# Weaving the feed-forward's down units into its up units, and twelve more seven-product units

## The chip, the core and the metric

The kernel runs on one core of a Trainium2 chip, with float32 inputs and outputs in HBM. The metric is the device time of one execution in microseconds (us). The engines are named as in the profile: PE (matrix products; PEld loads its stationary operand), DVE (vector), ACT (scalar), POOL, and SP, which issues most of the transfers. Each takes its own instructions strictly in the order written here, since the kernel is scheduled by hand; semaphores tie the engines together.

## What is computed

A decoder trunk of two layers over 256 tokens of width 2048. Each layer is a mixer (pooling in layer 0, attention in layer 1), a normalization, a gated feed-forward network with a short causal convolution, and another normalization:

```python
def conv_ffn(h, w_up, conv_w, conv_b, w_down):
    u = h @ w_up                          # 256x2048 @ 2048x11008
    up = jnp.pad(u, ((0, 0), (CONV_WIDTH - 1, 0), (0, 0)))
    c = conv_b + up[:, 0:S] * conv_w[0]
    for j in range(1, CONV_WIDTH):
        c = c + up[:, j:j + S] * conv_w[j]
    gate, val = jnp.split(c, 2, axis=-1)
    return (jax.nn.silu(gate) * val) @ w_down     # 256x5504 @ 5504x2048

def reference(x, ...):
    ...
        h = layer_norm(DEEPNORM_ALPHA * h + mix, ln1_g[i], ln1_b[i])
        ff = conv_ffn(h, ffn_w_up[i], ffn_conv_w[i], ffn_conv_b[i], ffn_w_down[i])
        h = layer_norm(DEEPNORM_ALPHA * h + ff, ln2_g[i], ln2_b[i])
```

The attention's masks depend on distances between tokens alone (three dilated windows), not on the inputs.

## The kernel before

**Units.** All large products are cut into units, kept in the list `units` and worked through by `run_units`. A unit is one block of weights of up to 512 rows by 512 columns (1 MB): SP loads it into `raw` (three buffers, line 72), ACT rounds it into `wh` (L82), DVE forms the rest `wl` (L83), and PE multiplies both by the activations, which are split in the same way. `wh` and `wl` have four buffers, so a unit's split can start once PE begins the unit three places ahead of it; `ahead(i)` writes the splits of units up to i+3 and the loads of units up to i+5 into the queues before unit i's matmuls. After these, `run_units` writes the functions that `later(n, fn)` has put off by n units, then the unit's own `post`. So "one step later" means "behind the next unit's split" on DVE and ACT.

**Up units.** A group of four up units (`group`, `mm_quad`, L165 and L166, tile `acc`) makes 512 features of the gate half or the value half, in four of the eight PSUM banks. Quads q = 0 to 10 each have a gate group and a value group (`up`). Then `evac` (L577, L578) empties the banks into `u` through the temporary `ut`, `conv` makes three taps in three steps (L586, L591, L592), the gate gets its sigmoid and product (L615, L616), and the value is multiplied by the gate (L670) and split into `gq[q]` by `split_act` (L287, L283).

**Down units.** The second matrix is taken in four chunks of quads, `chunks` = (0,1,2), (3,4,5), (6,7), (8,9,10), in token-major form by `down` and `group_tm`. Each chunk makes four groups c, one for each 512 output columns, with one item for each quad. A plain item (`mk`, `go_t`, L235 to L237, tile `t`) is 24 matmuls of 512 columns. A seven-product item replaces the eight block products of a 2x2 by 2x2 block product by seven, with sums of blocks: 42 matmuls of 256 columns (L224 to L226, tiles `t` and `s`), in two units "a" and "b" that share one load. `split_sums` makes the sums of the weight blocks in `raw` on DVE (L104, L107 to L109) along with their splits (L103, L106, L96, L97). `left_sums(q)` makes the sums of the activation blocks once for each q (L645 to L648, L654, L656) in one of two sets of buffers, A and B. Which quads take seven products is in `sevens`: q = 1, 2, 4, 5, 6 in layer 0, and also 7, and half of the groups of 9, in layer 1. That is 46 items. After a group, `early_post` and `tm_post` (L791 to L821) combine its four banks into the residual `HT`; part of that goes by accumulating DMAs from POOL (L268).

**Order.** The three first quads' up groups come first. From then on whole down groups stand between whole up groups: gates 3, group 0 of chunk 0, values 3, group 1, gates 4, group 2, values 4, group 3, then quad 5, and the same with chunk 1 between quads 6 and 7. Chunk 2's groups follow values 8, gates 9, values 9 and gates 10. The last chunk comes behind values 10: `add_last` in layer 0, token-major with an alternating order (`turns`) in layer 1. `free[q]` and `done[q]` name the unit behind which quad q's split and convolution may be written.

**Masks.** `masks(i)` (L1118 to L1132) makes three 128x128 tables with POOL's iota and ten DVE operations each, at units 61, 63 and 65 of layer 0's feed-forward stage; the attention's scores read them.

Of the kernel before, what the change touches and what calls it, by code (L numbers as in the profile page):

```python
# [9 lines left out]
F32 = mybir.dt.float32  # L10
# [22 lines left out]
def trunk(ctx: ExitStack, tc: tile.TileContext, x, pool_w_in, pool_w_grp, pool_scale, pool_w_out,  # L33
# [14 lines left out]
    def bank(nm):  # L48
        return psp.tile([P, 512], F32, name=nm, tag="ps")
# [40 lines left out]
    def split_sums(i, kind):  # L90
        h = wh[i] = wp.tile([P, 4, 512], F32R, name=f"wh{i}", tag="wh")
        l = wl[i] = wp.tile([P, 4, 512], F32R, name=f"wl{i}", tag="wl")
        if kind == "b":
            r = raw.pop(i - 1)
            for n in (N2, N1):
                A.copy(h[:, :, n], r[:, :, n])  # L96
                V.tensor_tensor(l[:, :, n], r[:, :, n], h[:, :, n].bitcast(F32), OP.subtract)  # L97
            return
        r = raw[i]
        r11, r12, r21, r22 = r[:, B1, N1], r[:, B1, N2], r[:, B2, N1], r[:, B2, N2]  # L100
# [3 lines left out]
        V.tensor_tensor(r12, r12, r11, OP.subtract)  # L104
# [3 lines left out]
        V.tensor_tensor(r21, r21, r22, OP.subtract)  # L108
        V.tensor_tensor(r11, r22, r11, OP.subtract)  # L109

# [78 lines left out]
    def group_tm(w, r0s, c0, ncol, xqs, post, apart=False, seven=(), early=None):  # L189
        ps, held = [], []  # L190

        def leave():
            early(*ps[2:4])

        opening, closing = (min(seven), max(seven)) if seven else (None, None)

        def mk_seven(kind, j):
            fst, fin, op, cl = j == 0, j == len(r0s) - 1, j == opening, j == closing

            def go(h, l):  # L200
# [38 lines left out]
        def mk(j):  # L239
            def go(h, l):  # L240
                if j == 0:
                    ps.extend([bank("t0"), bank("t1")])
                    if apart:
                        ps.append(bank("t2"))
# [51 lines left out]
    onesd = const.tile([P, P], F32, name="onesd")  # L296
    one1 = const.tile([P, P], F32, name="one1")
# [4 lines left out]
    cnt = const.tile([P, 3, P], F32, name="cnt")  # L302
    negm = const.tile([P, 3, P], F32, name="negm")

# [243 lines left out]
    def ffn(lay):  # L548
# [16 lines left out]
        def evac(ps, nb, mode):  # L565
# [3 lines left out]
            def tmp():  # L569
                return fp.tile([P, T], F32, name="ut", tag="t1", bufs=4)  # L570

# [53 lines left out]
        def left_sums(q, s):  # L625
            pool, tag = (hp, "h") if q in (2, 5, 7) else (lnp, "sq")
            two = pool.tile([P, 2, 2, 2, P], F32R, name="xs01", tag=tag)
# [4 lines left out]
            if q in (2, 5, 7):  # L632
                one = apart()
            else:
                one = pools["ffn"].tile([P, 2, 2, P], F32R, name="xs2", tag="xs", bufs=1)
                one = [one[:, 0], one[:, 1]]
# [28 lines left out]
        def val_chain(q, nb, mode, ps):  # L665
# [21 lines left out]

        def up(q, mid, end):
            nb = min(4, NF - 4 * q)
            x0 = q == 0  # L690
            mode = "x" if x0 else "ab"
            group(w_up, rows4, 512 * q, nb * P, psrcs if x0 else xsrcs, gate_post(q, nb, mode),
                  mode=mode)
            for g in mid:
                units.extend(g)
            group(w_up, rows4, FF + 512 * q, nb * P, xsrcs, val_post(q, nb, "ab"))
            for g in end:
                units.extend(g)

        def down(n, last):  # L700
            qs = order[chunks[n][0]]
            rows = [(512 * q, min(512, FF - 512 * q)) for q in qs]
# [11 lines left out]
        for q in range(3):  # L714
            up(q, (), ())
# [12 lines left out]
        free[9] = len(units) - 5  # L728
        mark = len(units)
# [78 lines left out]
    def tm_post(lay, n, c):  # L808
# [3 lines left out]
        def post(t, ps, half=None):  # L812
# [11 lines left out]
            if c == 0 and t == 0:  # L824
                ST["bn"] = lnp.tile([P, 2, 8, 6], F32, name="bn", tag="bn")
            for i in range(2) if half is None else (half,):
# [121 lines left out]
    def scores(hq, ms):  # L948
        ap = pools["attn"]
        for m in ms:  # L950
# [6 lines left out]
            s = two[:, m % 2]  # L957
            sf, nf, cf = (t.rearrange("p a b -> p (a b)") for t in (s, negm, cnt))
            V.scalar_tensor_tensor(sf, ps[:, :3 * P], scale, nf, op0=OP.mult, op1=OP.add)
# [8 lines left out]
        for m in ms:  # L968
            s, mx, _ = pr[hq, m]
            sf, cf = (t.rearrange("p a b -> p (a b)") for t in (s, cnt))  # L970
            for t, sl in parts:
# [64 lines left out]

    with tc.tile_pool(name="start", bufs=1) as stp:
        for q in range(NQ):
            for t in range(2):
# [73 lines left out]
    with tc.tile_pool(name="ffn0", bufs=4) as fp:  # L1113
        pools["ffn"] = fp


        def masks(i):
            two = fp.tile([P, 2, P], F32, name="dist", tag="t1", bufs=4)  # L1118
# [3 lines left out]
            itwo = fp.tile([P, 2, P], I32, name="idist", tag="t1", bufs=4)  # L1122
            idist, im = itwo[:, 0], itwo[:, 1]
            cn = cnt[:, i, :]
            V.tensor_copy(idist, dist)
# [5 lines left out]
            V.scalar_tensor_tensor(cn, dist, 0.0, cn, op0=OP.is_ge, op1=OP.mult)  # L1131
            V.tensor_scalar(negm[:, i, :], cn, 0.0, NEG, op0=OP.is_equal, op1=OP.mult)  # L1132

        for i in range(3):
            later(61 + 2 * i, lambda i=i: masks(i))
        run_units(marks[1])
    with tc.tile_pool(name="attn", bufs=1) as ap:
        pools["attn"] = ap
        run_units(marks[2])
# [32 lines left out]
```

## Time and profile before

| | |
|---|---|
| three runs | 2040.13, 2040.58, 2041.29 us; median 2040.58 |
| the profiled execution | 2042.79 us, of which 2041.0 us is the span from the first to the last instruction |
| granted PE clock, mean | 0.998 |
| layer 0's feed-forward up to its last chunk | 218 to 869 us of the span |
| attention stage | 933 to 1317 us |
| layer 1's feed-forward up to its last chunk | 1317 to 1966 us |
| DVE and ACT busy over the span | 1648.8 us (81%), 1235.0 us (61%) |
| loads of one 1 MB block, issue to landing | 5.0 to 5.5 us, median by tensor |

The profile is of one execution. A window row gives, for a stretch of time, the busy time and number of instructions of each engine, the granted PE clock, the share of the DMA engines and GB/s. A timeline row gives the start, the duration (us), engine, line, operation, tiles, and in brackets the idle time of the engine before it with what ended it. Matmuls overlap, so the price of one is the distance from its start to the next start, not its duration; the same holds to a smaller degree for DVE and ACT, whose recorded durations reach some 0.1 us into the next instruction.

### The profile page before, as it was taken

Reading aid. Unit: us, or ns where it says so; the run is one execution under the profiler, and the core shown is the slowest. Engines: PE = TensorE matmul, PEld = TensorE weight load, DVE = VectorE, ACT = ScalarE, POOL = GpSimd, SP = SyncE. Lnnn points to the kernel's source line nnn. Section 1 sums busy time; section 2 is a strip of 40 time slices with the busy share of each in tenths; the row PEclk is TensorE's granted clock in tenths of the full one; section 3 lists DMA queues with packets and bytes.
Section 4 is the critical chain, followed back from the end, with each engine's and each line's share of the span. In section 5 each row is a group of like instructions: output and inputs, shape, how many; then the busy total and the mean of one; then the engine's idle time right before and its main releaser. Section 6 shows DMA issues by size and latency. Waiting matters only on the chain. (4 is left out here: it accounts for less than half of the span.)

```text
span 2041.0 us, 30664 instructions
## 1 busy us (share of the span) xinstructions
PE 2029.8 (99%) x12316; PEld 1805.3 (88%) x12316; DVE 1648.8 (81%) x1973; ACT 1235.0 (61%) x1634; POOL 75.2 (4%) x112
## 2 busy tenths in 40 slices
PE   9999999999999999999999999999999999999999
PEld 8898988889889888889888888998898889889987
DVE  6859877988998888889755667787888878889998
ACT  5544686656766575657444344587765666567662
POOL 2000000000000001100000000000001000000100
PEclk9999999999999999999999999999999999999999
DMA  8655567656665667865556555557667646765764
GB/s 255 208 202 189 166 209 212 189 195 215 205 194 189 219 211 199 239 217 162 187 193 202 176 170 176 178 188 224 185 187 230 223 147 227 216 196 177 221 209 167
DMA packets 278302, 405.88 MB, mean 199 GB/s; under 512 B 80414, under 2 KB 95668, under 8 KB 277904
## 3 DMA queue, kind: packets, MB, share of 16 engines
q1 hardware_dynamic: 266144, 389.72, 58.4%
q0 software_dynamic: 11584, 13.55, 4.4%
q8 instruction: 96, 1.57, 0.3%
q10 hardware_dynamic: 432, 0.66, 0.1%
q14 instruction: 46, 0.38, 0.1%
HBM read 380.01 MB, written 2.10 MB: 187 GB/s over the span
## 5 line engine op out<-in xcount | busy, mean ns | idle before, releaser
L165 PE MATMUL acc<-xc,wh 128*128 128x512 f32 x3264 | 1150.3, 396 | 0.0
L166 PE MATMUL acc<-xc,wl 128*128 128x256 f32 x3264 | 915.9, 281 | 0.4 <-DVE wl L83 0.4
L83 DVE TENSOR_TENSOR wl<-raw,wh 128x2048 fp32r<-128x2048 f32 (+2 forms) x330 | 713.8, 2171 | 238.8 <-ACT wh L82 233.0
L82 ACT CAST wh<-raw 128x2048 fp32r<-128x2048 f32 (+2 forms) x330 | 596.5, 1814 | 279.7 <-PE acc L165 136.5
L165 PEld LDWEIGHTS acc<-xc,wh 128*128 128x128 f32 x3264 | 615.9, 189 | 144.7 <-DVE o L1024 0.6
L166 PEld LDWEIGHTS acc<-xc,wl 128*128 128x128 f32 x3264 | 615.4, 189 | 0.9 <-DVE wl L83 0.7
L96 ACT CAST wh<-raw 128x1024 fp32r<-128x1024 f32 x92 | 93.3, 1050 | 146.5 <-PE acc L165 69.4
L97 DVE TENSOR_TENSOR wl<-raw,wh 128x1024 fp32r<-128x1024 f32 x92 | 108.8, 1219 | 38.6 <-ACT wh L96 38.5
L103 ACT CAST wh<-raw 128x1024 fp32r<-128x1024 f32 x92 | 72.2, 834 | 49.8 <-PE acc L165 42.9
L586 ACT ACTIVATE c<-u,cv 128x256 f32<-128x256 f32 x172 | 89.6, 593 | 12.5 <-DVE f L648 8.2
L577 ACT COPY ut<-acc 128x256 f32<-128x256 f32 x164 | 56.3, 371 | 67.4 <-PE acc L166 67.2
L236 PE MATMUL t<-wl,g 128*128 128x512 f32 (+1 forms) x243 | 93.9, 387 | 1.9 <-DVE wl L83 1.9
L235 PE MATMUL t<-wh,g 128*128 128x512 f32 (+1 forms) x243 | 94.6, 389 | 0.8 <-ACT wh L82 0.8
L237 PE MATMUL t<-wh,g 128*128 128x512 f32 (+1 forms) x243 | 94.0, 387 | 0.0
L268 POOL DMA_DIRECT2D ht<-w x24 | 20.3, 848 | 1842.9 <-DVE ht L817 1106.6
L106 DVE TENSOR_TENSOR wl<-raw,wh 128x1024 fp32r<-128x1024 f32 x92 | 83.7, 951 | 0.2 <-ACT wh L103 0.2
L591 ACT ACTIVATE a<-u,cv 128x256 f32<-128x256 f32 x172 | 73.4, 498 | 7.0 <-DVE g L656 7.0
L578 DVE TENSOR_TENSOR u<-acc,ut 128x256 f32<-128x256 f32 x164 | 60.2, 414 | 21.0 <-ACT ut L577 21.0
L225 PE MATMUL t<-wl,g 128*128 128x256 f32 x272 | 76.4, 281 | 0.0
L224 PE MATMUL t<-wh,g 128*128 128x256 f32 x272 | 76.4, 281 | 0.0
L226 PE MATMUL t<-wh,g 128*128 128x256 f32 x272 | 76.3, 281 | 0.0
L591 ACT ACTIVATE u<-u,cv 128x256 f32<-128x256 f32 x172 | 73.4, 499 | 0.0
(274 smaller groups left out, 3398.1 us busy)
## 6 DMA issues: line engine op xcount, KB each, us to landing
raw<-in_ffn_w_up_dram SPq DMA_DIRECT2D x160, 1024.0 KB, 5.1
raw<-in_ffn_w_down_dram SPq DMA_DIRECT2D x80, 1024.0 KB, 5.2
raw<-in_pool_w_out_dram SPq DMA_DIRECT2D x16, 1024.0 KB, 5.0
raw<-in_shared_w_k_dram SPq DMA_DIRECT2D x16, 1024.0 KB, 5.0
raw<-in_attn_w_q_dram SPq DMA_DIRECT2D x16, 1024.0 KB, 5.2
raw<-in_shared_w_v_dram SPq DMA_DIRECT2D x16, 1024.0 KB, 5.3
raw<-in_attn_w_o_dram SPq DMA_DIRECT2D x16, 1024.0 KB, 5.0
raw<-in_pool_w_in_dram SPq DMA_DIRECT2D x12, 1024.0 KB, 5.5
```

What stands on the lines that cost most here:

```text
L82: A.copy(wh[i][:, s], r[:, s])
L83: V.tensor_tensor(wl[i][:, s], r[:, s], wh[i][:, s].bitcast(F32), OP.subtract)
L96: A.copy(h[:, :, n], r[:, :, n])
L97: V.tensor_tensor(l[:, :, n], r[:, :, n], h[:, :, n].bitcast(F32), OP.subtract)
L106: V.tensor_tensor(l[:, k, n], r[:, k, n], h[:, k, n].bitcast(F32), OP.subtract)
L165: PE.matmul(ps[m], h[:, k, c], q[:, k, :, :T], start=st, stop=False)
L166: PE.matmul(ps[m][:, :T], l[:, k, c], q[:, k, 0, :T], start=False, stop=sp and not shifted)
L235: PE.matmul(to, xh, h[:, k, c], start=j == 0 and k == 0, stop=False)
L236: PE.matmul(to, xh, l[:, k, c], start=False, stop=False)
L237: PE.matmul(to, xl, h[:, k, c], start=False, stop=j == len(r0s) - 1 and k == nk - 1)
L586: A.activation(c[:, m, :], u[:, m, 2:], AF.Identity, scale=cv[:, 2, j:j + 1], bias=cv[:, 3, j:j + 1])
L591: A.activation(to[:, m, :], u[:, m, i:i + T], AF.Copy, scale=cv[:, i, j:j + 1])
```

## The change

The order of the work is changed, and `sevens` is larger. A down group is no longer a block between two up groups: `weave` puts its items between the units of one up group. With three items the order is item, up, item, up, item, up, up; with two it is item, up, up, item, up, up. A seven-product item keeps its units a and b together. The four banks of a down group are opened at its first item (`opened`). Chunk 2's groups now go with values 8, gates 9, values 9 and gates 10.

Quads 1 to 7 take seven products in both layers (9 as before), so there are 58 such items: quads 3 and 7 in layer 0 and quad 3 in layer 1 are new. A third set C of buffers for the left sums is made in the feed-forward's pool. Room for it comes from the mask tables, which are now tiles of the attention stage, made there at steps 6 to 8, from one buffer less for `ut`, and from two small tiles that share or leave their place. `split_sums` does two subtractions in one instruction, and `left_sums` turns the sign of one sum to match. In layer 1 the convolution of the last value group is put off by one unit.

```diff
@@ split_sums
         V.tensor_tensor(r22, r22, r12, OP.subtract)
-        V.tensor_tensor(r21, r21, r22, OP.subtract)
-        V.tensor_tensor(r11, r22, r11, OP.subtract)
+        both = r[:, :, N1].rearrange("p (b k) n -> p b k n", b=2)
+        V.tensor_tensor(both, both, r22.unsqueeze(1).to_broadcast([P, 2, 2, 256]), OP.subtract)
@@ group_tm
+        def opened():
+            ps.extend([bank("t0"), bank("t1")])
+            if seven:
+                ps.extend([bank("s2"), bank("s3")])
...
                 if kind == "a" and fst:
-                    ps.extend([bank("t0"), bank("t1")])
-                if kind == "a" and op:
-                    ps.extend([bank("s2"), bank("s3")])
+                    opened()
@@ ffn
-        order = {0: (0, 1, 2), 3: (3, 4, 5), 6: (6, 7) if lay == 1 else (7, 6), 8: (8, 9, 10)}
         every = (0, 1, 2, 3)
-        sevens = {1: every, 2: every, 4: every, 5: every, 6: every}
+        sevens = {q: every for q in range(1, 8)}
+        sets = {1: "A", 2: "B", 3: "C", 4: "A", 5: "B", 6: "A", 7: "BC"[1 - lay], 9: "A"}
         if lay == 1:
-            sevens.update({7: every, 9: (0, 2)})
-        free, done = {}, {}
+            sevens[9] = (0, 2)
+        free = {}
...
-                return fp.tile([P, T], F32, name="ut", tag="t1", bufs=4)
+                return fp.tile([P, T], F32, name="ut", tag="t1", bufs=3)
@@ left_sums
+            where = sets[q]
+            fp = pools["ffn"]
+            pool, tag = {"A": (lnp, "sq"), "B": (hp, "h"), "C": (fp, "xsc")}[where]
...
-            V.tensor_tensor(d[2], a11, a21, OP.subtract)
+            V.tensor_tensor(d[2], a21, a11, OP.subtract)
@@ val_chain
-            after(done.get(q, state["done"] + (0 if q in (2, 5, 10) else 1)), lambda: conv(u, NF + 4 * q, nb, valued, q == 10))
+            after(state["done"] + (0 if q in (2, 5) or (q == 10 and lay == 0) else 1), lambda: conv(u, NF + 4 * q, nb, valued, q == 10))
@@ ffn, the order
+        def weave(us, ks):
+            items = []
+            for k in ks:
+                if len(k) > 3 and k[3] == "b":
+                    items[-1].append(k)
+                else:
+                    items.append([k])
+            last = None
+            for i, u in enumerate(us):
+                j = i if len(items) > 2 else i // 2 if i % 2 == 0 else len(items)
+                if j < len(items):
+                    units.extend(items[j])
+                    last = len(units) - 1
+                units.append(u)
+            return last
...
         for n in (0, 1):
             d = down(n, False)
             q = chunks[n + 1][0]
-            up(q, d[:1], d[1:2])
-            up(q + 1, d[2:3], d[3:])
-            free[q] = done[q + 1] = len(units) - 1
+            for us, ks in zip(up(q) + up(q + 1), d):
+                free[q] = weave(us, ks)
             if n == 0:
-                up(q + 2, (), ())
+                for us in up(q + 2):
+                    units.extend(us)
         d = down(2, False)
-        up(8, (), d[:1])
-        up(9, d[1:2], d[2:3])
-        up(10, d[3:], ())
-        free[9] = len(units) - 5
+        gates8, vals8 = up(8)
+        units.extend(gates8)
+        gates10, vals10 = up(10)
+        for us, ks in zip((vals8,) + up(9) + (gates10,), d):
+            free[9] = weave(us, ks)
+        units.extend(vals10)
@@ masks, now behind the opening of the attention's pool
+        for nm in ("cnt", "negm"):
+            ST[nm] = ap.tile([P, 3, P], F32, name=nm)
...
         for i in range(3):
-            later(61 + 2 * i, lambda i=i: masks(i))
-        run_units(marks[1])
+            later(6 + i, lambda i=i: masks(i))
```

More of the change, by code (lines that the diff above doesn't have):

```diff
@@ L241, in go @@
                 if j == 0:
-                    ps.extend([bank("t0"), bank("t1")])
+                    opened()
                     if apart:
@@ L686, in at, with up @@
             later(max(u - state["done"], 1), fn)
-        def up(q, mid, end):
+        def up(q):
             nb = min(4, NF - 4 * q)
@@ L691, in up @@
             mode = "x" if x0 else "ab"
+            mark = len(units)
             group(w_up, rows4, 512 * q, nb * P, psrcs if x0 else xsrcs, gate_post(q, nb, mode),
                   mode=mode)
-            for g in mid:
-                units.extend(g)
             group(w_up, rows4, FF + 512 * q, nb * P, xsrcs, val_post(q, nb, "ab"))
-            for g in end:
-                units.extend(g)
+            us = units[mark:]
+            del units[mark:]
+            return us[:4], us[4:]
+        def weave(us, ks):
[13 more added lines that the diff above has]
+            return last
         def down(n, last):
-            qs = order[chunks[n][0]]
+            qs = range(*chunks[n])
             rows = [(512 * q, min(512, FF - 512 * q)) for q in qs]
@@ L714, in ffn @@
         for q in range(3):
-            up(q, (), ())
+            for us in up(q):
+                units.extend(us)
         for n in (0, 1):
@@ L1114, in trunk @@
         pools["ffn"] = fp
+        run_units(marks[1])
+    with tc.tile_pool(name="attn", bufs=1) as ap:
+        pools["attn"] = ap
+        for nm in ("cnt", "negm"):
+            ST[nm] = ap.tile([P, 3, P], F32, name=nm)
         def masks(i):
-            two = fp.tile([P, 2, P], F32, name="dist", tag="t1", bufs=4)
+            two = ap.tile([P, 2, P], F32, name="dist", tag="t1", bufs=2)
             dist, fm = two[:, 0], two[:, 1]
```

28 lines of the change are left out of this document (12 added, 16 removed).

## The prediction

> **What bounds the kernel now.** I read the totals first, then who waits for whom on PE, then the timeline of PE for prices, then windows over single stages, and last the timelines of DVE and ACT where DVE is fullest.
>
> ```profile
> PE 2029.8 (99%) x12316; PEld 1805.3 (88%) x12316; DVE 1648.8 (81%) x1973; ACT 1235.0 (61%) x1634; POOL 75.2 (4%) x112
> ```
>
> The waits of PE, in us in total, how often, and the longest:
>
> ```profile
> PE t L236 <- DVE wl L83: 1.9, 1, 1.9
> ...
> PE t L235 <- ACT wh L82: 0.8, 1, 0.8
> ```
>
> PE is busy for all of the span and waits for others for a few us in total. So time is saved by giving PE less to do, and lost where DVE and ACT can no longer keep ahead of it. What a down item costs PE is the distance between starts:
>
> ```profile
> 1672.79 0.39 PE L235 MATMUL t<-wh,g 128*128 128x512 f32 x1
> ...
> 1678.38 0.28 PE L224 MATMUL s<-wh,g 128*128 128x256 f32 x1
> ...
> 1683.34 0.28 PE L224 MATMUL s<-wh,g 128*128 128x256 f32 x1
> ```
>
> The first pair of starts is a plain item (5.59 us), the second a seven-product item, a and b (4.96). How full DVE is beside them:
>
> ```profile
> 551.50:589.50 38.00, 38.00 (x239) 34.04 (x238) 33.89 (x44) 29.54 (x46) 0.00 (x0) 1.00 0.45 146
> 589.50:627.40 37.90, 37.90 (x238) 33.95 (x237) 32.15 (x36) 24.18 (x32) 2.61 (x3) 1.00 0.66 207
> ...
> 1890.30:1922.70 32.40, 32.40 (x215) 29.56 (x214) 31.03 (x36) 23.35 (x35) 2.58 (x3) 1.00 0.69 203
> ```
>
> The numbers after the stretch's length are PE, PEld, DVE, ACT and POOL. The second row is one up group and one down group of a plain and two seven-product items (32.15 us of DVE in 37.9); the first is the same while the left sums of quad 5 are made; the third is four up units and two seven-product items in layer 1, where DVE is idle for only 32.40 - 31.03 = 1.4 us and PE still runs through. DMA at 0.45 to 0.69 has room.
>
> **The change, part by part.** *Twelve more seven-product items* (quads 3 and 7 in layer 0, quad 3 in layer 1, four groups each): 12 x (5.59 - 4.96) = **-7.6 us** on PE, which sets the end.
>
> *Weaving* by itself takes no matmul away. What it can save is the waits that are there now because a whole down group drains DVE's lead:
>
> ```profile
> 1857.14 0.40 PE L165 MATMUL acc<-xc,wh 128*128 128x512 f32 x1
> 1857.95 0.38 PE L166 MATMUL acc<-xc,wl 128*128 128x256 f32 x1 [0.42 <-DVE wl L83]
> ...
> 1976.78 0.28 PE L226 MATMUL s<-wh,xs 128*128 128x256 f32 x1
> 1977.88 0.50 PE L235 MATMUL t<-wh,g 128*128 128x512 f32 x1 [0.83 <-ACT wh L82]
> 1980.27 0.50 PE L236 MATMUL t<-wl,g 128*128 128x512 f32 x1 [1.89 <-DVE wl L83]
> ```
>
> ```profile
> 1977.50:1980.94 3.44, 1.17 (x4) 0.77 (x5) 3.44 (x3) 3.22 (x4) 0.00 (x0) 1.00 0.00 0
> 1980.94:1984.35 3.41, 3.41 (x10) 2.66 (x9) 3.41 (x3) 1.39 (x2) 0.00 (x0) 0.50 0.78 262
> ```
>
> At 1857, behind layer 1's first group of two seven-product items, the distance is 0.81 us; a 512-column matmul costs a 24th of a plain item, 0.23. With chunk 2's items apart this goes: -0.6. At 1977, behind layer 1's last value group, the distances are 1.10 and 2.39 against 0.12 (a 42nd of 4.96) and 0.23, so 3.1 us are lost, and then 3.41 us run at clock 0.50, which loses 1.7: 4.8 in all. The cause stands on ACT:
>
> ```profile
> 1972.05 1.59 ACT L586 ACTIVATE c<-u,cv 128x256 f32<-128x256 f32 x3 [0.82 <-DVE u L578]
> ...
> 1975.94 1.89 ACT L82 CAST wh<-raw 128x2048 fp32r<-128x2048 f32 x1
> ```
>
> The last value group's nine convolution instructions (1972.05 to 1975.94) stand ahead of the cast that PE waits for. The change puts that convolution behind the cast (one unit later in layer 1). The cast then starts 3.9 us earlier and PE finds its block; quad 10's activations, now late instead, are needed only after another plain item. I take all 4.8; nothing if DVE is then so late that the cast isn't the last to come.
>
> *What DVE has to do in the woven groups.* The prices, by distances of starts:
>
> ```profile
> 1665.88 0.69 DVE L108 TENSOR_TENSOR raw<-raw 128x512 f32<-128x512 f32 x1
> 1666.50 0.68 DVE L109 TENSOR_TENSOR raw<-raw 128x512 f32<-128x512 f32 x1
> 1667.10 1.22 DVE L283 TENSOR_TENSOR g<-c,g 128x1024 fp32r<-128x1024 f32 x1
> 1668.23 0.42 DVE L645 TENSOR_TENSOR f<-c 128x256 f32<-128x256 f32 x1
> ...
> 1669.70 2.35 DVE L97 TENSOR_TENSOR wl<-raw,wh 128x1024 fp32r<-128x1024 f32 x2
> 1671.97 0.68 DVE L656 TENSOR_TENSOR xs<-f,xs 128x512 fp32r<-128x512 f32 x1
> ...
> 1673.26 0.41 DVE L578 TENSOR_TENSOR u<-acc,ut 128x256 f32<-128x256 f32 x1
> ...
> 1887.82 2.29 DVE L83 TENSOR_TENSOR wl<-raw,wh 128x2048 fp32r<-128x2048 f32 x1 [1.30 <-ACT wh L82]
> 1890.03 1.22 DVE L592 TENSOR_TENSOR c<-c,a 128x1024 f32<-128x1024 f32 x1
> ...
> 1902.75 0.68 DVE L104 TENSOR_TENSOR raw<-raw 128x512 f32<-128x512 f32 x1
> ...
> 1909.49 0.69 DVE L104 TENSOR_TENSOR raw<-raw 128x512 f32<-128x512 f32 x1
> ```
>
> A plain split costs 2.21 (1887.82 to 1890.03), a seven-product split 6.74 (1902.75 to 1909.49), an operation over 1024 elements 1.13. Two subtractions in one cost 1.13 instead of 1.22 (1665.88 to 1667.10): -0.09 for each item.
>
> The tight place is chunk 1, quads 3, 4 and 5, now all seven-product. Per woven group PE needs 37.9 - 0.63 = 37.3 us. DVE needs 32.15 + 6.74 - 2.21 - 3 x 0.09 = 36.4. There are four such groups in a layer. DVE may thus idle 0.9 us in a group; in the fullest stretch now it idles 1.4, because it stands behind ACT (the 1.30 at 1887.82). By that row PE waits 0.5 us in each group. A higher bound adds up two gaps: the 1.30, and a wait for the first load of the next group, whose buffer comes free only two plain splits (4.4 us) before it is wanted and whose transfer takes 5.2:
>
> ```profile
> raw<-in_ffn_w_down_dram SPq DMA_DIRECT2D x80, 1024.0 KB, 5.2
> ```
>
> That is 1.3 + 0.8 - 0.9 = 1.2 us. The lower bound is 0. I take 0.6, near the row of the whole stretch, for three groups in each layer: **+3.6 us**.
>
> The first of the four is worse, since quad 5's value chain, which had a gate group to run beside, now runs beside seven-product items:
>
> ```profile
> 1650.31 0.40 PE L165 MATMUL acc<-xc,wh 128*128 128x512 f32 x1
> ...
> 1650.78 2.08 ACT L586 ACTIVATE c<-u,cv 128x256 f32<-128x256 f32 x4
> 1652.76 1.90 ACT L82 CAST wh<-raw 128x2048 fp32r<-128x2048 f32 x1
> ```
>
> Count from the end of values 5 (1650.31). ACT is free for the next split at 2.45 us; with half a cast DVE can go on at 3.4. Until the third up unit's split is done it has two seven-product splits (13.3, of which L104's 0.6 goes ahead), two plain ones (4.4), two taps, a product and a split of 1.13 each (4.5), the left sums (1.47, from 1668.23 to 1669.70) and their splits (1.29, from 1671.97 to 1673.26): 24.4, so it ends at 27.8. PE comes there at 3 x 4.96 + 2 x 5.61 = 26.1 (an up unit is a quarter of 37.9 less 5.59 and 9.92). PE wants `wl` 0.23 later: 1.5 us late, a little more if the sums of quad 5, written behind a split, are met first. I take 1.8 for each layer (0 to 3): **+3.6 us**. Chunk 0's first group has the same chain beside a plain item in place of a seven-product one: DVE needs 6.74 - 2.21 = 4.5 us less over the same stretch, and PE takes 0.6 more. No wait there.
>
> *Edits costed at nothing.* The four down banks opened at once, and the next up group's banks taken after one item: their evacuation ends 1.3 us after DVE comes to it (1673.26, four of 0.33), under the 4.96 of the item between. If DVE is over 3 us late there, that wait adds to the ones above. One `ut` less: the fourth copy waits for the first addition, hidden by the same item. Set C and the sign cost no instruction. SP's loads come in the new order, two per 10.6 us of item and up unit instead of one per 5.6.
>
> *Masks* leave layer 0's feed-forward (no wait there now) for the attention's start, ten DVE operations and an iota each:
>
> ```profile
> 517.00:520.00 3.00, 2.32 (x11) 1.00 0.94 147
> ...
> 956.60:979.00 22.40, 22.40 (x127) 19.35 (x126) 17.96 (x19) 15.23 (x23) 0.00 (x0) 1.00 0.55 187
> 979.00:1002.00 23.00, 23.00 (x106) 18.92 (x105) 20.33 (x42) 12.15 (x16) 0.00 (x0) 1.00 0.58 199
> ```
>
> The first row, DVE alone, holds the first mask: at most 2.32 us, 7 for three. DVE has 4.4 and 2.7 us free in the two stretches. They are queued ahead of the evacuation of the first keys and queries, for which the first scores' matmuls on PE wait. I take +0.4 (0 to 1.5).
>
> **The sum**: -7.6 - 0.6 - 4.8 + 3.6 + 3.6 + 0.4 = -5.4 us. The profiled execution took 2042.8 (span 2041.0 and 1.8 around it), so it would take 2037.4; it lies 2.2 above the median of the runs, and from 2040.6 the forecast is **2035** us, 0.27% faster.
>
> **The rivals.** *No new wait*: DVE and ACT stay ahead in chunk 1 after all. For it speaks that DVE's sum is under PE's in three of four groups; against it the 1.4 us idle of the fullest stretch. Time: 2040.6 - 13.0 = 2028.
>
> *The gain is eaten*: the upper bounds hold, 6 x 1.2 + 2 x 3 + 1.5 = 14.7 against 13.0, so 2042; with half of the waits over my values 2040. For it speaks that the margin is 0.9 us in 37.
>
> *Slower*: the hand-over inside the seven-product split. DVE makes the sums, ACT casts them, DVE takes the rest:
>
> ```profile
> 1717.68 1.23 DVE L97 TENSOR_TENSOR wl<-raw,wh 128x1024 fp32r<-128x1024 f32 x1 [1.48 <-ACT wh L96]
> ```
>
> DVE waits 1.48 us here. Three of these in a group of chunk 1 make 36.4 + 4.4 = 40.8 against 37.3: 3.5 in each of eight groups, 28 us, so 2056. It decides from some 2.5 us idle in a group on (0.9 and 13.0/8). Against it: at 1902.75 the next item follows with no wait, since ACT there needn't wait for PE to free a buffer, and DVE that is behind finds buffers free.
>
> One more row bears on its price: in the stretch 1977.50 to 1980.94 PE was busy 1.17 of 3.44 us, and the next 3.41 ran at 0.50. The Trainium skill ("TensorE: Matmul & The Clock Gate", on HAM oscillation) lets the clock drop only after a gap of over some 3.4 us; by that rule these waits would cost no more than themselves, and the trace disagrees, since gaps of 0.83 and 1.89 us were enough. By the row alone each of the eight groups could lose another 1.7 us, 14 in all.
>
> **How the numbers follow.** Forecast (2031 to 2039) 0.47, no new wait 0.18, gain eaten (2039 to 2045) 0.18, slower 0.17. Less than about 0.2% (4.1 us) can't be told from no change here. The forecast's own range lies two thirds below 2036.5, so faster gets 0.18 + 0.32 = 0.50, the same 0.32, slower 0.18. The range reaches from just under the first rival (2027) to 2047, which takes in the upper bounds with the 4.8 us at the end not won.
>
> **What would show it.** Right: down items at 4.96 between up units at 5.61; no gaps at layer 1's first chunk-2 group and behind its last value group, no half clock there; PE waits for `wl` and the left sums only in chunk 1, longest in its first group. Wrong: waits in chunk 0 or 2, on banks, on loads, or in the attention's first scores; or the 3 us behind the last value group still there.

## The result, and the profile after

| | median of the runs, us | ratio to the kernel before (95% interval) |
|---|---|---|
| before | 2040.43 (6 runs, 2039.55 to 2041.29) | 1 |
| after | 2048.86 (6 runs, 2045.96 to 2050.95) | 1.0038 (1.0027 to 1.0048) |

The change makes the kernel slower by 0.4%; 2035 was forecast. The profiled execution of the changed kernel took 2047.57 us (span 2045.8), against 2042.79 (2041.0) before: 4.8 us more, where the medians lie 8.4 apart. Before's profiled execution lies 2.4 us above its median and after's 1.3 below. The half clock has a part in this. Before's profiled execution runs at it from 11.45 to 14.86, and by 30 us it is 1.9 us behind after's. It runs at it again from 1980.94 to 1984.35, which costs 1.7 and doesn't happen in every execution. After's is at full clock from 10.56 to 2044.91. The last section returns to this. Executions at a mean clock of 1.000 took 2039.35 to 2039.79 us before, and 2045.96 and 2047.57 after.

In the changed kernel, seven-product matmuls are L227 to L229, plain items L238 to L240, the splits of activations L286, of left sums L658; the lines up to L109 are as before. Its totals and PE's waits:

```profile
PE 2027.3 (99%) x12532; PEld 1810.4 (88%) x12532; DVE 1699.9 (83%) x2020; ACT 1259.2 (62%) x1679; POOL 75.2 (4%) x112
```

```profile
PE acc L166 <- DVE wl L83: 5.4, 8, 2.0
PE t L229 <- DVE g L658: 2.3, 4, 0.7
PE s L228 <- DVE wl L97: 2.1, 3, 1.5
PE acc L165 <- DVE xc L286: 1.6, 1, 1.6
```

Sixteen waits of 11.4 us in all have taken the place of the three of 3.1 (1.9, 0.8 and 0.4) that the kernel before had behind its start. A wait costs a little more than the idle time in its row, since durations overlap. Summed over all matmuls with 0.233 us for 512 columns and 0.1185 for 256, PE's work at full rate has indeed gone down, by 7.4 us; but what the distances of starts add to that rate has gone up by 12.2 us.

**Won as forecast.** The cast behind layer 1's last value group now stands ahead of the convolution, and PE runs through at full clock (timeline of ACT, then the window over the same place):

```profile
1979.88 1.93 ACT L82 CAST wh<-raw 128x2048 fp32r<-128x2048 f32 x1
1981.75 1.59 ACT L586 ACTIVATE c<-u,cv 128x256 f32<-128x256 f32 x3
```

```profile
1977.50:1984.50 7.00, 7.00 (x43) 6.18 (x42) 7.00 (x9) 7.00 (x13) 0.00 (x0) 1.00 0.39 131
```

**Lost in chunk 1.** One woven group of layer 0, first the window from one wait of PE to the next, then DVE's timeline over a period of the same group:

```profile
605.04:643.51 38.47, 37.97 (x257) 34.51 (x255) 36.04 (x40) 25.79 (x35) 2.58 (x3) 1.00 0.64 206
```

```profile
603.46 2.29 DVE L83 TENSOR_TENSOR wl<-raw,wh 128x2048 fp32r<-128x2048 f32 x1 [0.58 <-ACT wh L82]
...
614.54 4.49 DVE L83 TENSOR_TENSOR wl<-raw,wh 128x2048 fp32r<-128x2048 f32 x2
619.77 0.69 DVE L104 TENSOR_TENSOR raw<-raw 128x512 f32<-128x512 f32 x1 [0.74 <-DMA raw<-in_ffn_w_down_dram]
620.86 1.83 DVE L106 TENSOR_TENSOR wl<-raw,wh 128x1024 fp32r<-128x1024 f32 x2 [0.40 <-ACT wh L103]
...
640.09 1.23 DVE L592 TENSOR_TENSOR c<-c,a 128x1024 f32<-128x1024 f32 x1 [0.38 <-ACT a L591]
641.89 2.29 DVE L83 TENSOR_TENSOR wl<-raw,wh 128x2048 fp32r<-128x2048 f32 x1 [0.58 <-ACT wh L82]
```

From L83 at 603.46 to the same step one group on at 641.89 DVE takes 38.4 us. It waits for 0.74 + 0.40 + 0.38 + 0.58 = 2.1 of them and works for 36.3, as the prediction had it (36.4). PE needs 37.3, so DVE's chain is what sets the period, and PE waits for it:

```profile
605.81 0.38 PE L166 MATMUL acc<-xc,wl 128*128 128x256 f32 x1 [0.37 <-DVE wl L83]
...
656.18 0.39 PE L166 MATMUL acc<-xc,wl 128*128 128x256 f32 x1 [0.87 <-DVE wl L83]
```

Behind values 5, in the first of the woven groups, PE first waits for the left sums and the split that follows them on DVE:

```profile
573.94 0.39 PE L229 MATMUL t<-wh,g 128*128 128x256 f32 x1 [0.70 <-DVE g L658]
575.07 0.39 PE L228 MATMUL s<-wl,xs 128*128 128x256 f32 x1 [0.27 <-DVE wl L97]
```

By distances of starts, the waits of at least 0.12 us are 0.86, 0.43, 0.29 behind values 5 and 0.54, 0.29, 0.50, 1.03, 0.25, 0.23 in the three groups behind in layer 0, 4.3 in the same places of layer 1: 8.7 in all.

**Lost elsewhere.** At chunk 0's first group of either layer PE waits for the own left sums. These are the last of the four sums, which `left_sums` keeps in the quad's own `g`; they stand last on DVE, behind the item's L97 (0.68 and 0.65 us by distances):

```profile
373.09 2.35 DVE L97 TENSOR_TENSOR wl<-raw,wh 128x1024 fp32r<-128x1024 f32 x2
375.36 0.68 DVE L658 TENSOR_TENSOR xs<-f,xs 128x512 fp32r<-128x512 f32 x1
375.96 0.42 DVE L658 TENSOR_TENSOR xs3Q<-f,xs3S 128x256 fp32r<-128x256 f32 x1
376.29 0.42 DVE L658 TENSOR_TENSOR g<-f,g 128x256 fp32r<-128x256 f32 x1
```

```profile
376.77 0.39 PE L229 MATMUL t<-wh,g 128*128 128x256 f32 x1 [0.52 <-DVE g L658]
```

Layer 0's chunk 2, where quad 7 is new, loses 4.5 us (0.63 at 782, 1.70 and 2.15 here). PE, then ACT, then DVE:

```profile
843.45 0.38 PE L228 MATMUL s<-wl,xs 128*128 128x256 f32 x1 [1.54 <-DVE wl L97]
```

```profile
848.64 0.38 PE L166 MATMUL acc<-xc,wl 128*128 128x256 f32 x1 [1.98 <-DVE wl L83]
```

```profile
831.00 0.37 ACT L577 COPY ut<-acc 128x256 f32<-128x256 f32 x1 [3.67 <-DVE u L578]
831.27 1.48 ACT L82 CAST wh<-raw 128x1536 fp32r<-128x1536 f32 x1
```

```profile
832.79 1.76 DVE L83 TENSOR_TENSOR wl<-raw,wh 128x1536 fp32r<-128x1536 f32 x1 [0.88 <-ACT wh L82]
835.58 1.25 DVE L798 STREAM_TRANSPOSE hb<-ht 128x1024 f32<-128x1024 f32 x1 [1.03 <-DMA ht<-u]
```

ACT's fourth copy has no `ut` until DVE, which is behind, has used the first; the cast stands behind the copy, DVE's split behind the cast. Over the whole span ACT waits so 38 times; in the list of waits before, L577 waited for PE's matmuls alone. First the changed kernel, then the one before:

```profile
ACT ut L577 <- DVE u L578: 117.2, 38, 5.8
```

```profile
ACT ut L577 <- PE acc L166: 67.2, 77, 1.1
```

In the attention's start the first mask (976.65 to 978.96) stands ahead of the second half of the normalised activations on DVE, and PE loses 1.76:

```profile
976.65 0.22 DVE L1152 CAST idist<-dist 128x128 int32<-128x128 f32 x1
...
978.82 0.23 DVE L1159 TENSOR_SCALAR negm<-cnt 128x128 f32<-128x128 f32 x1
978.96 1.22 DVE L286 TENSOR_TENSOR xc<-h,xc 128x1024 fp32r<-128x1024 f32 x1
```

```profile
980.33 0.47 PE L165 MATMUL acc<-xc,wh 128*128 128x512 f32 x1 [1.60 <-DVE xc L286]
```

### The profile page after: what moved, and what is told of

Its sections match the earlier page's. It is cut to its first block, busy times and chain, and to the rows that moved or that the text cites. A ratio compares the mean times of both kernels' runs of the same rounds, so it can differ in the third digit from the quotient of the medians.

```text
span 2045.8 us, 31252 instructions
## 1 busy us (share of the span) xinstructions
PE 2027.3 (99%) x12532; PEld 1810.4 (88%) x12532; DVE 1699.9 (83%) x2020; ACT 1259.2 (62%) x1679; POOL 75.2 (4%) x112
## 5 line engine op out<-in xcount | busy, mean ns | idle before, releaser
L83 DVE TENSOR_TENSOR wl<-raw,wh 128x2048 fp32r<-128x2048 f32 (+2 forms) x318 | 686.7, 2167 | 241.3 <-ACT wh L82 240.5
L82 ACT CAST wh<-raw 128x2048 fp32r<-128x2048 f32 (+2 forms) x318 | 572.9, 1810 | 249.9 <-PE acc L165 124.8
L96 ACT CAST wh<-raw 128x1024 fp32r<-128x1024 f32 x116 | 121.0, 1052 | 88.3 <-DVE raw L107 76.3
L97 DVE TENSOR_TENSOR wl<-raw,wh 128x1024 fp32r<-128x1024 f32 x116 | 137.2, 1219 | 7.7 <-ACT wh L96 7.7
L577 ACT COPY ut<-acc 128x256 f32<-128x256 f32 x164 | 55.0, 370 | 139.9 <-DVE u L578 117.2
L103 ACT CAST wh<-raw 128x1024 fp32r<-128x1024 f32 x116 | 90.8, 831 | 56.0 <-DMA raw<-in_ffn_w_down_dram 36.3
L106 DVE TENSOR_TENSOR wl<-raw,wh 128x1024 fp32r<-128x1024 f32 x116 | 105.6, 952 | 8.2 <-ACT wh L103 8.1
L229 PE MATMUL t<-wh,g 128*128 128x256 f32 x344 | 96.8, 281 | 2.3 <-DVE g L658 2.3
L228 PE MATMUL t<-wl,g 128*128 128x256 f32 x344 | 96.8, 281 | 0.0
L227 PE MATMUL t<-wh,g 128*128 128x256 f32 x344 | 96.7, 281 | 0.0
L228 PE MATMUL s<-wl,xs 128*128 128x256 f32 x308 | 86.8, 282 | 2.1 <-DVE wl L97 2.1
L227 PE MATMUL s<-wh,xs 128*128 128x256 f32 x308 | 86.1, 280 | 0.0
L229 PE MATMUL s<-wh,xs 128*128 128x256 f32 x308 | 86.0, 279 | 0.0
L109 DVE TENSOR_TENSOR raw<-raw 128x1024 f32<-128x1024 f32 x58 | 71.1, 1225 | 2.0
```

The costliest lines, as they stand in the source:

```text
L82: A.copy(wh[i][:, s], r[:, s])
L83: V.tensor_tensor(wl[i][:, s], r[:, s], wh[i][:, s].bitcast(F32), OP.subtract)
L227: PE.matmul(to, xh, h[:, k, n], start=opens and kk == 0, stop=False)
L228: PE.matmul(to, xh, l[:, k, n], start=False, stop=False)
L229: PE.matmul(to, xl, h[:, k, n], start=False, stop=ends and kk == 1)
```

## The experiments

All medians are of 4 to 11 runs; ratios are to the kernel before on the same chip, whose median there was 2041.1 (first four kernels), 2041.4 (next four), 2041.1 and 2041.0 us. "After" has 1.0038 on this scale.

### Which of the changes costs what

**46 units, woven.**

```diff
-        sevens = {q: every for q in range(1, 8)}
+        sevens = {q: every for q in (1, 2, 4, 5, 6)}
...
-            sevens[9] = (0, 2)
+            sevens[7], sevens[9] = every, (0, 2)
@@ down
-            qs = range(*chunks[n])
+            qs = (7, 6) if n == 2 and lay == 0 else range(*chunks[n])
```

> The changed kernel with the 46 seven-product units of before: quad 3 in both layers and quad 7 in layer 0 go back to plain items. Theory (the 12 added seven-product items fill DVE and ACT, and that is where PE's new waits come from): the waits in chunk 1 of both layers (5.3 and 5.0 us in the profile of the changed kernel) and in layer 0's chunk 2 (4.5) are gone, the 7.6 us of matmuls come back, and what is left against before is -0.6 and -4.8 at layer 1's end, +1.8 in the attention (masks) and +1.3 behind chunk 0's two first groups: about 2038, up to 2042 when counted from the changed kernel's time. Rival (the woven order, with its three ut buffers and its order of loads, makes the waits whatever the items are): they stay, and the time is 2049 + 7.6 = 2056.

Measured: 2040.54, ratio 0.9999 (0.999 to 1.0008). PE's waits:

```profile
PE acc L165 <- DVE xc L286: 1.6, 1, 1.6
PE t L229 <- DVE g L658: 1.4, 3, 0.7
```

The waits for `wl` in chunk 1 and chunk 2 are gone, so the theory holds. With 46 units the order and the other edits together are worth nothing: what they win at layer 1's end they give back to the masks (1.7 by distances) and the left sums (2.2 at the first groups of chunks 0 and 1).

**Quad 3 plain** in both layers, 50 units.

```diff
-        sevens = {q: every for q in range(1, 8)}
+        sevens = {q: every for q in (1, 2, 4, 5, 6, 7)}
```

> The changed kernel with quad 3 plain in both layers, so 50 seven-product units. Theory: PE's waits in chunk 1 (10.3 us in both layers) are gone and 8 x 0.63 = 5.0 us of matmuls come back: 2049 - 5.3 = 2043.6; the waits of layer 0's chunk 2 (4.5) stay. Rival (the weaving makes the waits): 2049 + 5 = 2054.

Measured: 2041.29, ratio 1.0001 (0.9992 to 1.001). In its profile chunk 1 has one wait of 0.38 and one of 0.33 us behind values 5. The eight items of quad 3 save 5.0 us of matmuls and cost about 12.6 us: without them the kernel is 0.37% (7.6 us) faster. Waits and smaller delays in chunk 1 make some 10.3 of these; where the rest comes from isn't shown.

**Quad 7 plain in layer 0**, and first in its items as in the first diff.

```diff
-        sevens = {q: every for q in range(1, 8)}
+        sevens = {q: every for q in range(1, 7)}
...
+            sevens[7], sevens[9] = every, (0, 2)
```

> The changed kernel with quad 7 plain in layer 0 and first in its items. Theory: the waits of layer 0's chunk 2 (0.63, 1.70 and 2.15 us, 4.5 in all) are gone and 4 x 0.63 = 2.5 us of matmuls come back: 2049 - 2.0 = 2047; the waits of chunk 1 stay. Rival (those waits come from the transposition of the finished quads, with its wait for a DMA on DVE and its sixteen moves on SP ahead of the weight loads, whatever the items are): 2049 + 2.5 = 2051.4, with at least 4 us of waits left there.

Measured: 2049.38, ratio 1.0041 (1.0028 to 1.0053). Inconclusive by its time, since the two expectations lie 4 us apart and it fell between. The three waits are gone from the trace, so the transposition alone doesn't make them. Whether they need the seven products of quad 7 or its place behind quad 6 wasn't tried apart. A new wait of 1.45 us ends at 730.25, where the split (L286) of quad 7, now first, ends at 730.20, too late for PE.

**The masks alone**, moved in the kernel before as the change does it.

```diff
-            later(61 + 2 * i, lambda i=i: masks(i))
...
     with tc.tile_pool(name="attn", bufs=1) as ap:
...
+            later(6 + i, lambda i=i: masks(i))
```

> The kernel before with one edit: the masks are made in the attention stage, after units 6, 7 and 8, in place of layer 0's feed-forward. Theory (the masks on DVE delay the split of the normalised activations, for which PE waits at the attention's start): before + 1.8 = 2042.2, with a wait of 1.6 us of PE acc for DVE xc near 978. The prediction's value: before + 0.4. Rival (that wait has another cause, a later start of the stage): before + 0.0.

Measured: 2042.95, ratio 1.0008 (1.0 to 1.0017). The theory holds: +1.9 us, though the interval reaches down to nothing, and the trace has the wait seen above:

```profile
PE acc L165 <- DVE xc L283: 1.6, 1, 1.6
```

**The last convolution alone**, in the kernel before.

```diff
-            after(done.get(q, state["done"] + (0 if q in (2, 5, 10) else 1)), lambda: conv(u, NF + 4 * q, nb, valued, q == 10))
+            after(done.get(q, state["done"] + (0 if q in (2, 5) or (q == 10 and lay == 0) else 1)), lambda: conv(u, NF + 4 * q, nb, valued, q == 10))
```

> The kernel before with one edit of one line: quad 10's convolution one unit later in layer 1. Theory (the gain at layer 1's end comes from this line alone and needs no weaving): the waits of 0.99 and 2.15 us at 1977 and the half clock that follows them in some runs are gone: before - 3.1 to - 4.8, so about 2037. Rival (quad 10's activations are then late for the item that takes them, or the cast isn't what comes last): before - 1 or no change.

Measured: 2037.02, ratio 0.9975 (0.9966 to 0.9985), 4.4 us. The theory holds: this line is the change's largest gain besides the matmuls, and it needs nothing of the rest. Of PE's waits in the feed-forward only the one at 1857 is left.

**58 units, not woven:** the items of each down group stand as a block behind their up group.

```diff
             for us, ks in zip(up(q) + up(q + 1), d):
-                free[q] = weave(us, ks)
+                units.extend(us)
+                units.extend(ks)
+            free[q] = done[q + 1] = len(units) - 1
```

> The changed kernel's 58 seven-product units with the down groups not woven: each stands as a block behind its up group, as before. Theory (weaving spreads DVE's 20.2 us of splits per down group of chunk 1; in a block DVE loses 20.2 - 14.9 = 5.3 us against PE and has to make them up from its lead): waits of 1.5 to 3 us behind each of the eight down groups of chunk 1 in place of 1.3, so 2053 to 2062. Rival (only the sum over the 37.3 us of a whole group matters, the order doesn't): 2049.

Measured: 2081.43, ratio 1.0192 (1.0178 to 1.0205), more than either expected. PE's waits:

```profile
PE acc L166 <- DVE wl L83: 14.8, 11, 2.0
PE s L228 <- DVE wl L97: 9.3, 7, 2.0
PE s L227 <- ACT wh L96: 5.1, 5, 2.2
```

So weaving is worth some 31 us once there are 58 units, while with 46 it and the rest of the change are worth nothing: it keeps DVE's lead from being used up in one block. Not all of it is waits in chunk 1, as the theory had it: waits of 1 to 2.3 us stand in chunk 2 as well, and five stretches at half clock between 582 and 1894 us cost 8.5 of the 31 us. A part may also be that convolutions there wait for the whole block, as before; that wasn't tried apart.

### What makes DVE late

**Evacuation in place.**

```diff
-                t = tmp()
-                A.copy(t, ps[m][:, T:])
-                V.tensor_tensor(u[:, m, 2:], ps[m][:, :T], t, OP.add)
+                A.copy(u[:, m, 2:], ps[m][:, T:])
+                V.tensor_tensor(u[:, m, 2:], ps[m][:, :T], u[:, m, 2:], OP.add)
```

> The changed kernel with the evacuation of the feed-forward's up groups made in place: ACT copies the right half of a bank into u itself and DVE adds the left half there, so there is no ut buffer for ACT to wait for. Nothing else is changed. Theory (ACT's waits for DVE over the three ut buffers, 38 of 5.8 us in all in the changed kernel's profile and none before, push the casts behind them late): those waits are gone, PE's waits at the head of each chunk-1 group (0.3 to 1.0 us, some 6 of the 10.3) and part of the 2.15 us near 846 shrink by half or more: 2049 - 4 = 2045. Rival (DVE has no time left there, and ACT's copy waits only because DVE is behind): within 1 us of the changed kernel's 2049.

Measured: 2044.04, ratio 1.001 (1.0001 to 1.0019). The size is the theory's, the place is not. At the head of chunk 1's groups the waits are what they were; the one at 656 as an example:

```profile
656.08 0.38 PE L166 MATMUL acc<-xc,wl 128*128 128x256 f32 x1 [0.86 <-DVE wl L83]
```

What went is 0.63 and 1.70 in layer 0's chunk 2 and half of the wait in each of chunk 0's first groups (0.35 and 0.32 left). In chunk 1 the `ut` buffers weren't the cause. These waits add up to 3.0 us and 1.0 is lost anew, at 898.66, where L362 waits for DVE; the profiled executions lie 2.2 us apart (spans 2045.8 and 2043.5), the medians 4.8. What makes the rest isn't shown. Fewer stretches at half clock may be part of it: no execution here has a mean clock under 0.999, and two of the changed kernel's six do.

**Own left sums first**, on top of it.

```diff
-                vs = [((two[:, :, 0], two[:, :, 1]), both), (xs[q][2], d[2]), (xs[q][3], d[3])]
+                vs = [(xs[q][3], d[3]), ((two[:, :, 0], two[:, :, 1]), both), (xs[q][2], d[2])]
```

> The kernel with the evacuation in place and one more edit: of the left sums' casts and splits the own ones, which the first seven-product unit takes first among them, are made first in place of last. Theory: the four waits of PE t for DVE g behind the quads' left sums (0.68, 0.65, 0.86 and 0.79 us) go: the kernel without this edit - 3.0, so 2042 if the evacuation in place is worth 4. Rival (the wait only moves to the next left sums, which are then 0.4 us later): - 1 or less.

Measured: 2042.78, ratio 1.0008 (0.9999 to 1.0017), not to be told from the one above. In the trace both hold, each in one place: chunk 0's two waits are gone, and behind values 5, where DVE is behind in any case, 0.80 and 0.44 became one wait of 1.34 for `wl` L97. One new wait, of 1.18 for `wl`, stands in layer 1 at 1947.34.

**Loads of seven-product units in two pieces**, on top of both. The first piece is all that DVE's and ACT's first instructions need.

```diff
@@ pieces
+        if len(units[i]) > 3:
+            return [B1, B2]
@@ split_sums
-        parts = [(slice(0, 4), N1), (B2, N2)]
+        parts = [(B1, N1), (B2, slice(0, 512))]
```

> The kernel with the evacuation in place and the own left sums first, and one more edit: the load of a seven-product unit is issued in two pieces of two row blocks each, and its first casts and splits are cut the same way, so that DVE's and ACT's first instructions wait for the first piece alone. The number of instructions on DVE and ACT stays. Theory (DVE is bound in chunk 1, 36.3 us of work in a period of 38.4, and of the 2.1 us in which it waits there some 1.2 are the wait for a load, 0.76, and for the cast behind it, 0.40, once in every woven group): DVE's wait for the load goes, and PE's waits of 1.3 us a group in chunk 1 fall to 0.3 or less: 2043 - 5 to - 7, so 2037. Rival (the wait is for the cast chain on ACT, and the second piece lands no earlier than the whole did): 2043 - 1 or no change.

Measured: 2038.94, ratio 0.9987 (0.9978 to 0.9997): 4 us won where 5 to 7 were expected. DVE's timeline at the place of the 0.74 and 0.40 above (lines up by two):

```profile
603.70 2.29 DVE L85 TENSOR_TENSOR wl<-raw,wh 128x2048 fp32r<-128x2048 f32 x1 [0.57 <-ACT wh L84]
...
614.77 4.49 DVE L85 TENSOR_TENSOR wl<-raw,wh 128x2048 fp32r<-128x2048 f32 x2
619.18 0.69 DVE L106 TENSOR_TENSOR raw<-raw 128x512 f32<-128x512 f32 x1
619.78 0.69 DVE L108 TENSOR_TENSOR wl<-raw,wh 128x512 fp32r<-128x512 f32 x1
621.25 1.23 DVE L108 TENSOR_TENSOR wl<-raw,wh 128x1024 fp32r<-128x1024 f32 x1 [0.78 <-ACT wh L105]
...
641.68 2.29 DVE L85 TENSOR_TENSOR wl<-raw,wh 128x2048 fp32r<-128x2048 f32 x1 [0.58 <-ACT wh L84]
```

Of the wait for the load and its cast (0.74 + 0.40 = 1.14) 0.78 are left, now for the second piece's cast; the period (603.70 to 641.68) falls from 38.4 to 38.0, and with it PE's wait of 0.5 us at each next group's first up unit is gone. With the smaller delays, what PE loses in chunk 1's groups behind the first falls from 1.2 to 0.8 us a group, where the theory had 0.3 or less. That is 2.6 us of the four. The waits of 1.41 in layer 0's chunk 2 and of 1.18 at 1947.34, which the theory didn't name, are gone too. For chunk 1 the reading stands: DVE's chain of 36.3 us of work and 2.1 of hand-overs is over PE's 37.3, and time taken from a hand-over is won by PE.

### A version that is faster than both

**All edits together**, with the masks back in layer 0's feed-forward, where the room of `ut` has become free; 58 units with the loads in two pieces, then 50 (quad 3 plain) with loads in one piece and in two.

```diff
+            four = lnp.tile([P, 4, P], F32, name="dist", tag="fold2")
...
+            later(61 + 2 * i, lambda i=i: masks(i))
         run_units(marks[1])
     with tc.tile_pool(name="attn", bufs=1) as ap:
         pools["attn"] = ap
-        for nm in ("cnt", "negm"):
-            ST[nm] = ap.tile([P, 3, P], F32, name=nm)
...
-            later(6 + i, lambda i=i: masks(i))
```

> All of it together, with 58 seven-product units and woven: evacuation in place, own left sums first, loads of seven-product units in two pieces, and the masks back in layer 0's feed-forward (their tiles fit where the ut buffers were; quad 0's evacuation takes its temporaries from buffers of the folds). Theory: the kernel with loads in two pieces - 1.9 for the masks, so 2035 if the pieces are worth 5 to 7; PE's wait at the attention's start is gone. Rival (the pieces are worth nothing): 2041.

Measured: 2036.25, ratio 0.9975 (0.9967 to 0.9984), near the theory.

> Evacuation in place, own left sums first, masks back in layer 0's feed-forward, woven, quad 3 plain in both layers (50 seven-product units), loads in one piece. Theory: the 50-unit kernel's 2041.3, - 1.9 for the masks, - 1.7 for the waits behind left sums and - 1 to - 2 in layer 0's chunk 2: 2036, about that of the kernel before with quad 10's convolution one unit later (2037). Rival (what is left in layer 0's chunk 2 comes back as half clock in many runs): 2039.

Measured: 2032.99, ratio 0.9961 (0.9948 to 0.9973), 3 us better than expected; where the 3 us come from wasn't worked out. In its profile PE has one wait of the feed-forward left:

```profile
PE acc L166 <- DVE wl L83: 0.2, 1, 0.2
```

> The 50-unit kernel of all edits with the loads of seven-product units in two pieces as well. Theory: without quad 3 DVE isn't bound in chunk 1, so there is nothing there for the pieces to win; the 0.39 us left in layer 0's chunk 2 may go: 2033 - 0.4. Rival (the additional loads on SP's queue cost something where nothing waits for them): 2034 to 2035.

Measured: 2032.76, ratio 0.9959 (0.9945 to 0.9972), the theory's value. So with the other edits made 50 units beat 58 by some 3 us: DVE has room for quad 7 but not for quad 3. Against the kernel before with only the last convolution put off (0.9975), the weaving, quad 7 and the mends gain 3 to 4 us.

## Why the prediction was wrong

The gains came nearly as predicted. The step that failed is the price of DVE's lateness: its terms in the sum, 7.6 us, came to 12.9 with the smaller delays, and 5.8 more lay in places that were costed at nothing, chunk 0 and layer 0's chunk 2.

- **Twelve items, -7.6**: right (7.4 at full rate). **The wait at 1857, -0.6**: right.
- **Layer 1's end, -4.8**: right in place, cause and about in size, shown by the one-line edit alone (-4.4). The 1.7 us of half clock in it belong only to some runs.
- **Chunk 1's first group, 1.8 in each layer**: right in its cause, a DVE that comes late, and in size, 1.6 and 1.5 (some 0.3 more in smaller delays). The places are others: the prediction counted the delay at the third up unit, and PE meets all of it earlier, 1.2 to 1.3 at the left sums and the split behind them, which it had taken for "a little more", and 0.3 at the first up unit. With the own left sums first it is 1.34 and 0.29, so the total hangs on DVE's work and the places on its order.
- **Chunk 1's other groups, 0.6 each, 3.6 in all**: the step that failed most within the sum. They cost 5.6 in waits of 0.12 us or more (2.8 a layer), and about 1.8 more in smaller delays, 7.4 in all or 1.2 a group. The prediction's own upper bound added the two hand-overs that stand in the trace (1.3 behind ACT and 0.8 for the load) and gave 1.2; it then took half, "near the row of the whole stretch". But the idle time of the stretch is an average over a DVE that mostly keeps ahead, while the hand-overs are links of the chain that each woven group goes through: DVE waits 2.1 us a group, and 36.3 + 2.1 - 37.3 = 1.1.
- **"No wait there" for chunk 0's first group**: wrong, 1.3 in all. The totals of DVE's work were right; what counts is the place in the queue, and the sums stand behind an L97 of 2.35 us with the one that PE wants first standing last.
- **"One `ut` less: ... hidden by the same item"**: wrong where DVE is behind already. ACT then waits for DVE, DVE for ACT's next cast: 2.3 us in layer 0's chunk 2, shown by the evacuation in place, where the waits of 0.63 and 1.70 are gone.
- **Layer 0's chunk 2** wasn't worked out at all beyond its gain of 2.5 us and lost 4.5. Besides the `ut`, the transpositions of the finished quads and the loads fall in it; which of these makes the remaining 2.2 is open. Of the terms put at nothing this is the largest. It is 1.4 with the own left sums first and gone with the loads in two pieces.
- **Masks, +0.4**: 1.8 in the trace, 1.9 by medians, over the bound of 1.5. The free time of DVE in a stretch of 22 us says nothing of an instruction that PE waits for: ten operations, 2.3 us together, stand directly ahead of it.

By waits of 0.12 us and more the new losses are 8.7 + 1.3 + 4.5 + 1.8 = 16.3 against 7.6 taken; some 3 us more lie in shorter delays, most of them in chunk 1. The difference of the spans, +4.8, is -7.4 - 0.6 - 3.1 - 3.6 + 16.3 + 3.2, where 3.6 is before's later start (1.9) and its half clock at 1981 (1.7), and 3.2 is what is left over. Without the 3.6 it is 8.4, like the medians; that the two agree so well is in part chance, since other executions of the changed kernel have half clock of their own.

**The rivals.** By its time the result lies midway between "the gain is eaten" (2042) and "slower" (2056). By its mechanism it is the first, with bounds that left out the last four points. The mechanism of "slower", three hand-overs of 1.48 us in each group of chunk 1, isn't in the trace: DVE's waits for the sums' casts (L96) went down. Before, then after:

```profile
DVE wl L97 <- ACT wh L96: 38.5, 27, 1.7
```

```profile
DVE wl L97 <- ACT wh L96: 7.7, 8, 2.4
```

The hand-over at the split's start (L106, for ACT's L103) went up from 0.2 to 8.1 us in all, once 0.40 in the group above. The fall agrees with the argument against the rival, that a DVE which is behind finds buffers free.

## What to carry to other kernels

When a second engine is brought to within some per cent of the bound, add up its work and each hand-over on its chain over one period: the idle time of today's stretch is not what hand-overs will cost when there is no lead. Then look at the order in its queue at each place where the lead is smallest, and count a buffer taken away as a wait of the producer for a consumer that is late. And take a large change apart: here one line was worth 4 us alone, and a part of the units with small mends beat both the kernel before and all of the units.

## What the runs showed of the hardware

The half clock behind a wait of PE is not certain. The masks-only kernel has the same two waits at layer 1's end as before (0.79 and 1.89 of idle time), and the clock stays full behind them. What decides it is where the waits fall in a fixed raster of time. In all fourteen traces every change of the granted clock lies a whole number of steps of 3.413 us from the others, to within 0.005 us, and a stretch at half clock ahead of the end lasts one step, 3.41 us. In the kernel before the stretches begin at 11.45, 1980.94 and 2038.96, which are 577 and 17 steps apart. The raster begins at another point in each execution.

In the kernel before nearly all of the two waits lies in the step up to 1980.94, with PE busy for 1.17 us of it (the row from 1977.50 in the prediction, but for 0.03 us). In the masks-only kernel, whose clock changes at 5.85 and 2040.19, the raster cuts the same waits in two:

```profile
1975.34:1978.75 3.41, 2.12 (x15) 1.60 (x13) 3.13 (x4) 3.19 (x5) 0.00 (x0) 1.00 0.19 72
1978.75:1982.16 3.41, 2.02 (x9) 1.67 (x10) 3.41 (x3) 3.41 (x4) 0.00 (x0) 1.00 0.25 43
```

The kernel with quad 3 plain, behind the waits of layer 0's chunk 2:

```profile
842.85:846.26 3.41, 1.43 (x8) 1.06 (x8) 3.41 (x3) 1.04 (x1) 0.00 (x0) 1.00 0.97 269
846.26:849.67 3.41, 3.41 (x13) 2.93 (x12) 2.19 (x3) 2.69 (x3) 0.00 (x0) 0.50 0.92 261
```

Behind the first 15 us and ahead of the end, the fourteen traces have seven such stretches, each behind a step in which PE is busy for 0.34 to 0.51 of the time. No step with 0.52 or more is followed by one, and neither are two with 0.47, one of them in the changed kernel, from 846.83 on, behind the same waits as here. The prediction's other 14 us, half clock behind each of the eight groups of chunk 1, stayed away: in the changed kernel's profile chunk 1's waits leave PE busy for 0.73 or more of every step. So the waits of one kernel cost 1.7 us more in some runs than in others: the changed kernel's six runs go from 2045.96 us at a mean clock of 1.000 to 2050.95 at 0.998. The Trainium skill ("TensorE: Matmul & The Clock Gate", on HAM oscillation) puts the drop behind a gap of over some 3.4 us. The longest distance of two starts ahead of the drops shown here is 2.4 us, so as a rule on single gaps it doesn't hold here; the stretches at half clock do have the length that it names.
